# The down projection of a gated feed-forward block by Strassen's algorithm, with its operand sums made ahead in the gate and up passes

## The chip, the core and the metric

The kernel runs on one core of one Trainium2 chip. The time is device microseconds of one execution: 2796.57 us, the median of 3 runs (2796.07 to 2796.67). A separate execution was profiled; it took 2792.36 us.

## The reference

One layer of a hybrid trunk over 16 meta tokens and 2048 tokens of width 1024, all in 32-bit floating point: a token mixer (a state-space branch and an mLSTM branch, merged and projected), and then a channel mixer. Only the channel mixer, and in it the last product, matters here:

```python
def channel_mixer(x, g_pre, g_post, w_gate, w_up, w_conv, b_conv, w_down):
    h = rmsnorm(x, g_pre)
    a = causal_dwconv(h @ w_gate, w_conv, b_conv)
    y = (jax.nn.gelu(a, approximate=True) * (h @ w_up)) @ w_down
    return x + rmsnorm(y, g_post)
```

The inner width is 2816, 22 blocks of 128 features. Shapes of the down projection: y is 2048 x 2816, w_down 2816 x 1024. The result is normalized over all 1024 features of a token, multiplied with g_post and added to x.

## The kernel before

TensorE multiplies 32-bit numbers in a rounded form (fp32r). To keep the precision, every operand is split into a high part, which ACT rounds (an activation Copy into an fp32r tile), and a low part, the rest, which DVE subtracts. Each product is then three matmuls: high x high, high x low, low x high (`mm3`, lines 172 to 174; `mm3x`, lines 177 to 179, is the same without a check on groups). So each operand tile costs a load, an ACT and a DVE instruction before TensorE can use it.

All DMAs of the kernel are issued by SP, one after the other, in SP's own order. Each waits there until its buffer is free or its data is written, and what stands behind it waits as well. The program text gives the dependencies and the buffers (a pool's tile with `bufs=2` has two buffers that take turns); a scheduler sets the order of each engine's instructions.

The channel mixer has two parts.

**Gate and up passes** (`ffn_unit`, called in two loops over the 22 feature blocks m; first for the token half p=0, then for p=1). Gate and up are computed together by Strassen's algorithm in Winograd's form: seven products in the order 1, 6, 2, 7, 5, 4, 3 in place of eight, each of 4 depth blocks. Their seven operand tiles of h lie in SBUF throughout a pass (t0 to t11, q0, q1, from `t4(i)` and `q4(i)`). The weights of a unit are loaded (wg at line 1131, wu at 1133, buffer `ws` of pool dw), summed on DVE (s1 to s4) and split (lines 1124, 1125). In pass p=0 the moving operand has 258 or 256 columns (two pieces whose products alternate), in pass p=1 512. Behind the products come sums in u1 to u3 and gp (DVE), a causal convolution along tokens (ACT line 1254, DVE line 1256 twice), gelu (ACT line 1257), the product with the up half (DVE line 1261), and a store into `y_d` (line 1262) in DRAM, twice a unit.

**Down projection** (after `phX.close()`). For each half nh of the output features (512 columns) the weights w_down of all 22 depth blocks lie in SBUF, split (loaded into tiles `mk`, split at lines 1328 and 1329 into the t tiles). Then over 16 token tiles i: three loads `ys` from y_d of 8, 8 and 6 depth blocks (line 1335), each split into `yhl` (lines 1338 and 1339), and 22 x 3 matmuls into one PSUM bank with y as the stationary operand and 512 columns of weights moving. ys and each part of yhl have two buffers. A square sum (ACT line 1345) and a product with g_post (DVE, 1347 or 1350) follow. The results of nh=0 stay in SBUF; with nh=1 the token is normalized, h1 is loaded and added, and the output stored (1355 to 1359).

## Time and profile before

| | |
|---|---|
| median of 3 runs | 2796.57 us |
| profiled execution, its time / its span | 2792.36 us / 2790.6 us |
| TensorE busy (PE) | 2759.1 us, 99% |
| DVE / ACT busy | 1761.1 us, 63% / 1054.7 us, 38% |
| gate and up, pass p=0 | from 1403.8 us to about 1850 us |
| gate and up, pass p=1 | from there to about 2290 us |
| down projection, first and last matmul | 2287.3 us, 2783.3 us |
| DMA traffic | 395.47 MB, mean 142 GB/s |

PE are TensorE's matmuls and PEld its weight loads, which overlap them. The duration of a single matmul is longer than the distance of two, since they are pipelined; the pace is read from counts over a stretch of time. DVE is VectorE, ACT ScalarE, POOL GpSimd, SP SyncE, whose queue issues the DMAs. In a row of a group there stand line, engine, operation, output and inputs by their names in the program, shapes and count, then busy time in us and mean ns of one, then idle time before it and what ended most of it.

### The profile page before, as it was taken

To read this page: it belongs to the slowest core of one execution; us is meant where nothing else is said; L and a number is where in the kernel's file an instruction comes from. 1 tells how busy PE (TensorE), PEld (TensorE's weight loads), DVE (VectorE), ACT (ScalarE), POOL (GpSimd) and SP (SyncE) were. 2 spreads that over 40 slices of the span, in tenths; PEclk is the share of its full clock that TensorE was granted. 3 is DMA by queue.
4 is the path that set the end of the run, shared out by engine and by line. 5 is a ranking of instruction groups with operands and counts; after the bars stand their busy time and mean duration, and the time that the engine had idled before them with its cause. 6 is when DMAs were issued, how large, how long until landed. Compare 5 with 4: busy or idle time off the path is not lost.

```text
span 2790.6 us, 40815 instructions
## 1 busy us (share of the span) xinstructions
PE 2759.1 (99%) x15590; PEld 2484.9 (89%) x15590; DVE 1761.1 (63%) x3429; ACT 1054.7 (38%) x1979; POOL 136.8 (5%) x225
## 2 busy tenths in 40 slices
PE   8999999999999999999999999999999999999999
PEld 8999999999999987777799999998788788888887
DVE  4637799377555464676798887786776683224333
ACT  6102344233444444344354434453443352224221
POOL 1000000000000000000100000000000000000000
PEclk9999999999999999999999999999999999999999
DMA  9333443212454574667744462252222244335453
GB/s 309 106 79 131 158 147 121 71 69 72 145 159 144 167 212 121 223 196 250 265 157 138 159 234 87 73 176 85 80 80 81 79 145 149 99 90 165 157 166 128
DMA packets 323478, 395.47 MB, mean 142 GB/s; under 512 B 40321, under 2 KB 229142, under 8 KB 322642
## 3 DMA queue, kind: packets, MB, share of 16 engines
q1 hardware_dynamic: 323282, 392.86, 43.9%
q8 instruction: 122, 2.00, 0.3%
q14 instruction: 74, 0.61, 0.1%
HBM read 284.47 MB, written 108.31 MB: 141 GB/s over the span
## 4 chain that ended last, share of the span: by engine, by line
PE 82%; DMA 7%; DVE 6%; ACT 1%; issue 1%; POOL 1%; SPq 0%; DVEq 0%; POOLq 0%; ACTq 0%
PE mm L172 10%; PE mm L174 10%; PE mm L173 10%; PE ac L173 9%; PE ac L174 9%; PE ac L172 8%; PE ac L179 4%; PE ac L178 4%; PE ac L177 4%; PE mm L177 3%; PE mm L179 3%; PE mm L178 3%; DMA wu<-in_w_up_dram 2%; DMA gat<-gab_d 1%; DVE w L1125 1%
## 5 line engine op out<-in xcount | busy, mean ns | idle before, releaser
L174 PE MATMUL mm<-hTh,wl 128*128 128x410 f32 (+3 forms) x1216 | 428.0, 352 | 0.0
L172 PE MATMUL mm<-hTh,wh 128*128 128x410 f32 (+3 forms) x1216 | 427.6, 352 | 0.0
L173 PE MATMUL mm<-hTl,wh 128*128 128x410 f32 (+3 forms) x1216 | 427.4, 352 | 0.0
L1339 DVE TENSOR_TENSOR yhl<-ys,yhl 128x1024 fp32r<-128x1024 f32 (+1 forms) x96 | 109.1, 1137 | 291.9 <-ACT yhl L1338 291.9
L173 PE MATMUL ac<-t,yhl 128*128 128x512 f32 x704 | 278.5, 396 | 0.0
L174 PE MATMUL ac<-t,yhl 128*128 128x512 f32 x704 | 277.3, 394 | 0.0
L172 PE MATMUL ac<-t,yhl 128*128 128x512 f32 x704 | 276.6, 393 | 0.0
L177 PE MATMUL mm<-t,w 128*128 128x258 f32 (+2 forms) x792 | 253.7, 321 | 3.5 <-DVE u L1226 2.6
L178 PE MATMUL mm<-t,w 128*128 128x258 f32 (+2 forms) x792 | 253.5, 320 | 0.4 <-DVE t L1069 0.4
L177 PE MATMUL ac<-t,w 128*128 128x258 f32 (+2 forms) x792 | 253.2, 320 | 0.6 <-ACT u L1217 0.6
L179 PE MATMUL ac<-t,w 128*128 128x258 f32 (+2 forms) x792 | 253.1, 320 | 0.1
L179 PE MATMUL mm<-t,w 128*128 128x258 f32 (+2 forms) x792 | 252.5, 320 | 0.7 <-DVE w L1125 0.7
L178 PE MATMUL ac<-t,w 128*128 128x258 f32 (+2 forms) x792 | 253.1, 320 | 0.0
L173 PEld LDWEIGHTS mm<-hTl,wh 128*128 128x128 f32 x1216 | 228.7, 188 | 2.6
L174 PEld LDWEIGHTS mm<-hTh,wl 128*128 128x128 f32 x1216 | 228.8, 188 | 2.3
L172 PEld LDWEIGHTS mm<-hTh,wh 128*128 128x128 f32 x1216 | 228.7, 188 | 2.0
L1338 ACT ACTIVATE yhl<-ys 128x1024 fp32r<-128x1024 f32 (+1 forms) x96 | 95.0, 990 | 348.4 <-PE ac L173 345.9
L156 ACT ACTIVATE wh<-ws 128x1024 fp32r<-128x1024 f32 x104 | 109.9, 1059 | 237.8 <-PE mm L173 137.5
L1124 ACT ACTIVATE w<-s 128x512 fp32r<-128x512 f32 x176 | 109.3, 628 | 164.7 <-DVE s L1139 70.3
L177 PEld LDWEIGHTS mm<-t,w 128*128 128x128 f32 x792 | 149.7, 189 | 18.0 <-DVE u L1226 4.4
L172 PEld LDWEIGHTS ac<-t,yhl 128*128 128x128 f32 x704 | 132.4, 188 | 32.3
L177 PEld LDWEIGHTS ac<-t,w 128*128 128x128 f32 x792 | 149.2, 189 | 13.0 <-ACT u L1217 1.1
(453 smaller groups left out, 6074.1 us busy)
## 6 DMA issues: line engine op xcount, KB each, us to landing
ys<-y_d SPq DMA_DIRECT2D x64, 512.0 KB, 3.7
wg<-in_w_gate_dram SPq DMA_DIRECT2D x44, 512.0 KB, 3.6
wu<-in_w_up_dram SPq DMA_DIRECT2D x44, 512.0 KB, 4.3
gab_d<-ev SPq DMA_DIRECT2D x80, 205.0 KB, 2.4
ws<-in_w_m_dram SPq DMA_DIRECT2D x32, 512.0 KB, 3.8
ws<-in_w_ba_dram SPq DMA_DIRECT2D x32, 512.0 KB, 4.0
ws<-in_w_out_dram SPq DMA_DIRECT2D x32, 512.0 KB, 5.3
gat<-gab_d SPq DMA_DIRECT2D x48, 256.0 KB, 4.8
```

Of the source, the lines that this page charges most:

```text
L156: S.activation(wh, ws, AF.Copy, scale=scale)
L172: T.matmul(out=ps, lhsT=lh, rhs=rh, start=first, stop=False)
L173: T.matmul(out=ps, lhsT=lh, rhs=rl, start=False, stop=False)
L174: T.matmul(out=ps, lhsT=ll, rhs=rh, start=False, stop=last)
L177: T.matmul(out=ps, lhsT=lh, rhs=rh, start=first, stop=False, skip_group_check=True)
L178: T.matmul(out=ps, lhsT=lh, rhs=rl, start=False, stop=False, skip_group_check=True)
L179: T.matmul(out=ps, lhsT=ll, rhs=rh, start=False, stop=last, skip_group_check=True)
L1124: S.activation(t[:, 0], src, AF.Copy)
L1125: V.tensor_tensor(t[:, 1], src, t[:, 0].bitcast(F32), ALU.subtract)
L1338: S.activation(yh, ys, AF.Copy)
L1339: V.tensor_tensor(yl, ys, yh.bitcast(F32), ALU.subtract)
```

## The change

The down projection becomes one Strassen step (Winograd's form, as in gate and up), over y in quarters: two token groups of 128 (j and j+4 of a pass), and the depth in two halves of 11 blocks. A `down_unit` computes two token tiles by 512 features with seven products, each of 11 depth blocks x 3 matmuls with 256 moving columns. There are 8 units for each feature half nh, so 2 x 8 x 7 products.

Three of the seven operands of y are parts of y itself, four are sums, and so it is for the weights. The sums are made earlier and put in DRAM: those of the weights (`down_weight_sums`, into `wt_d`) in the first gate and up pass, one call in each of the units m = 9 to 20, two loads, four DVE sums and four stores; those of y (`down_input_sums`, into `s_d`) in the second pass, one call in each of the units m = 1 to 11 and 13 to 21, again two loads of 512 KB from y_d, four DVE sums of 128x512 and four stores of 256 KB. For two of the depth blocks the sums of the second token half are made within the down projection, after its second and third unit (j = 1 and 2; `late_sums`).

For every feature half the seven weight operands lie in SBUF, 8 of their 11 depth blocks in the t and q tiles (`main`), 3 in tiles x1 to x7 (`rest`). For nh=0 the mains of five products are loaded and split within the last gate and up unit (`turn_down`), the other two and all rests in the first down unit; those of nh=1 in the last unit of nh=0 and the first of nh=1 (the table `cut`). Each stationary operand (704 KB), each main piece, each rest piece and the late sums use one tag `raw` with two buffers in the new pool dn, which takes over the space of dw, mk, du and dx. The results of nh=0 go to DRAM (`yo_d`) and are loaded again by `finish`.

```diff
+    def down_weight_sums(nh, k):
+        kn = min(2, 11 - k)
+        t = mk_tile()[:, 0:kn * 1024].rearrange("p (k b n) -> p k b n", k=kn, b=4)
...
+        V.tensor_tensor(b11, b12, b11, ALU.subtract)
...
+    def down_input_sums(p, m, t1, t2):
+
+        for h, t in ((0, t1), (1, t2)):
+            P.dma_start(out=t, in_=y_d[m + 11 * h, :, p * 1024:(p + 1) * 1024])
+        a11, a21, a12, a22 = t1[:, 0:512], t1[:, 512:1024], t2[:, 0:512], t2[:, 512:1024]
+        V.tensor_tensor(a22, a21, a22, ALU.add)
+        V.tensor_tensor(a21, a11, a21, ALU.subtract)
+        V.tensor_tensor(a11, a22, a11, ALU.subtract)
+        V.tensor_tensor(a12, a12, a11, ALU.subtract)
+        for i, a in enumerate((a11, a21, a12, a22)):
+            P.dma_start(out=s_d[p * 4:p * 4 + 4, i, :, m, :].rearrange("j p t -> p j t"),
+                        in_=a.rearrange("p (j t) -> p j t", j=4))
...
+        if 9 <= m < 21:
+            down_weight_sums((m - 9) // 6, (m - 9) % 6 * 2)
...
     for m in range(NF):
         if m:
             wt = weights_second(*weights(m))
-        ffn_unit(1, m, op1, wt)
+        i = m - 1 if m < 12 else m - 13
+        if i >= 0 and i < (11 if m < 12 else 9):
+            t = mk_tile()
+            down_input_sums(int(m > 12), i, t[:, 0:1024], t[:, 1024:2048])
+        ffn_unit(1, m, op1, wt, turn_down if m == NF - 1 else None)
     phX.close()
+    phM.close()
+    phW.close()
...
+    dn = pool(ctx, "dn")
+
+    def raw_tile():
+        return dn.tile([128, 1408], F32, tag="raw", name="raw", bufs=2)
...
+    def stationary(j, n):
+        raw = raw_tile()
+        src3 = raw.rearrange("p (m t) -> p m t", m=11)
+        if n in (1, 2, 4):
+            c0 = j // 4 * 1024 + j % 4 * 128 + 512 * (n == 4)
+            m0 = 11 * (n != 1)
+            P.dma_start(out=src3, in_=y_d[m0:m0 + 11, :, c0:c0 + 128].rearrange("m p t -> p m t"))
+        else:
+            P.dma_start(out=src3, in_=s_d[j, {6: 0, 7: 1, 3: 2, 5: 3}[n]])
+        turn_[0] += 1
+        st = dn.tile([128, 2, 1408], F32R, tag=f"st{turn_[0] % 2}", name="st")
+        S.activation(st[:, 0], raw, AF.Copy)
+        V.tensor_tensor(st[:, 1], raw, st[:, 0].bitcast(F32), ALU.subtract)
+        return st.rearrange("p a (m t) -> p a m t", m=11)
...
+        def prod(ps, n, first):
+            for f in before.get(n, ()):
+                f()
+            st = ahead.pop(n, None) or stationary(j, n)
+            for k in range(11):
+                mm3x(ps, st[:, 0, k], st[:, 1, k], moving(n, 0, k), moving(n, 1, k), first and k == 0, k == 10)
...
+    def second(n):
+        return [lambda: main_piece(1, n, 0), lambda: main_piece(1, n, 4), lambda: rest_split(1, n)]
+
+    todo = [f for n in ORDER for f in second(n)]
+
+    cut = [0, 0, 1, 3, 5, 6, 8, 9, 12, 14, 16, 18, 20, 21]
+    for j in range(8):
+        if j == 0:
+            before = first
+        elif j == 7:
+            before = {n: todo[cut[i - 1] if i else 0:cut[i]] for i, n in enumerate(ORDER)}
+        else:
+            before = {}
+        down_unit(0, j, g4, before)
+        if j in (1, 2):
+            late_sums(8 + j)
```

How the order of SP's queue changes, at two places. Rows show line, the tile written and the one read; waits are named by the engine that gives the semaphore (DVE, Activation, PE) or by the DMA queue's (DMAHW). Line numbers of the changed program differ: y_d<-cc is line 1262 before and 1297 after, wg 1131 and 1166, wu 1133 and 1168.

The first place is the second gate and up pass. Before, a unit's rows on SP are these four:

```order
L1262 DMA y_d<-cc 128x512 [waits DMAHW2_49,DVE_49]
L1262 DMA y_d<-cc 128x512 [waits DMAHW3_49,DVE_49]
L1131 DMA wg<-in_w_gate_dram 128x1024 [waits DMAHW0_49,DVE_49,Activation_49]
L1133 DMA wu<-in_w_up_dram 128x1024 [waits DMAHW1_49,DVE_49]
L1262 DMA y_d<-cc 128x512 [waits DMAHW6_49,DVE_49]
```

After, in a unit past the twelfth (mk<-y_d are the loads of y for the sums, s_d<-mk the stores of the sums):

```order
L1297 DMA y_d<-cc 128x512 [waits DMAHW5_49,DVE_49]
L1147 DMA mk<-y_d 128x1024 [waits DMAHW5_49,DMAHW3_49]
L1154 DMA s_d<-mk 128x4x128 [waits DMAHW6_49,DVE_49]
L1166 DMA wg<-in_w_gate_dram 128x1024 [waits DVE_49,Activation_49]
L1154 DMA s_d<-mk 128x4x128 [waits DVE_49]
L1154 DMA s_d<-mk 128x4x128 [waits DMAHW2_49,DVE_49]
L1154 DMA s_d<-mk 128x4x128 [waits DVE_49]
```

A load that waits for DMA queues only (its own y block must have been stored) and a store of a sum now stand between the store of y and the load of the next unit's wg.

The second place is the beginning of the down projection. Before, the loads of y (ys) stand among the last stores of the gate and up units:

```order
L1335 DMA ys<-y_d 128x8x128 [waits DMAHW4_49,DVE_49,Activation_49]
L1322 DMA mk<-in_w_down_dram 128x4x512 [waits DVE_49]
L1335 DMA ys<-y_d 128x8x128 [waits DMAHW5_49,DMAHW2_49,DVE_49]
L1262 DMA y_d<-cc 128x512 [waits DMAHW3_49,DVE_49]
L1322 DMA mk<-in_w_down_dram 128x4x512 [waits DVE_49]
L1335 DMA ys<-y_d 128x6x128 [waits DMAHW0_49,DVE_49]
L1322 DMA mk<-in_w_down_dram 128x2x512 [waits DMAHW6_49,DVE_49]
L1262 DMA y_d<-cc 128x512 [waits DMAHW7_49,DVE_49]
```

After, the first load of a stationary operand (raw<-y_d) stands behind the last three stores, and the loads that follow go to the two raw buffers in turn:

```order
L1297 DMA y_d<-cc 128x512 [waits DVE_49] x3
L1397 DMA raw<-y_d 128x11x128 [waits DMAHW6_49,PE_49]
L104 DMA g_23166<-in_g_ffn_post_dram 128x512
L1399 DMA raw<-s_d 128x1408 [waits DMAHW0_49,PE_49]
L1495 DMA ht<-h_d 128x512 [waits DMAHW3_49,DMAHW1_49,Pool_49]
L1495 DMA ht<-h_d 128x512 [waits DMAHW2_49]
L1411 DMA raw<-in_w_down_dram 128x3x256 [waits DMAHW6_49,DVE_49]
L1411 DMA raw<-wt_d 128x768 [waits DMAHW4_49,DMAHW0_49,DVE_49]
L1411 DMA raw<-in_w_down_dram 128x3x256 [waits DMAHW5_49,DMAHW3_49,DVE_49]
L1397 DMA raw<-y_d 128x11x128 [waits DMAHW4_49,DVE_49]
L1411 DMA raw<-wt_d 128x768 [waits DMAHW7_49,DMAHW5_49,DVE_49]
L1399 DMA raw<-s_d 128x1408 [waits DMAHW6_49,DVE_49]
```

Rests (line 1411) and stationaries (1397, 1399) alternate; every raw load from the third on waits for DVE, which reads the buffer last.

More of the change, by code (lines that the diff above doesn't have):

```diff
@@ L86, in mixer_ffn_kernel @@
     y_d = dp.tile([NF, 128, 2048], F32, name="y_d")
+    s_d = dp.tile([8, 4, 128, 11, 128], F32, name="s_d")
+    wt_d = dp.tile([2, 4, 128, 11, 256], F32, name="wt_d")
+    yo_d = dp.tile([16, 128, 512], F32, name="yo_d")
     win_d = dp.tile([8, 128, 512], F32, name="win_d")
@@ L858, in mixer_ffn_kernel @@
         mlstm(pool(ph, "ml", bufs=2))
-    mk = pool(ctx, "mk")
+    phM = ExitStack()
+    mk = pool(phM, "mk")
     def mk_tile(dt=F32):
@@ new lines, in rest_tile, with rest_split, main_piece @@
+    def rest_tile(n):
+        wrest[n] = dn.tile([128, 2, 768], F32R, tag=f"x{n}", name=f"x{n}")
+    def rest_split(nh, n):
+        raw = raw_tile()[:, 0:768]
+        P.dma_start(out=raw.rearrange("p (k n) -> p k n", k=3), in_=down_src(nh, n, 8, 11))
+        rest_tile(n)
+        S.activation(wrest[n][:, 0], raw, AF.Copy)
+        V.tensor_tensor(wrest[n][:, 1], raw, wrest[n][:, 0].bitcast(F32), ALU.subtract)
+    def main_piece(nh, n, k0):
+        raw = raw_tile()[:, 0:1024]
+        P.dma_start(out=raw.rearrange("p (k n) -> p k n", k=4), in_=down_src(nh, n, k0, k0 + 4))
+        if k0 == 0:
+            places(n)
+        main_split(n, k0, raw.rearrange("p (a n) -> p a n", a=2))
@@ new lines, in finish @@
+    def finish(t, o1):
+        sm = dn.tile([128, 1], F32, tag="sm", name="sm", bufs=2)
+        V.tensor_reduce(out=sm, in_=sq4[t], op=ALU.add, axis=mybir.AxisListType.X)
+        rs = rstd_of(Small(dn, "r", 2), sm, 128, 1, 1.0 / D)
+        o0 = dn.tile([128, 512], F32, tag="o", name="o0", bufs=3)
+        P.dma_start(out=o0, in_=yo_d[t])
+        for hh, src in ((0, o0), (1, o1)):
+            cs_ = slice(hh * 512, hh * 512 + 512)
+            ht = dn.tile([128, 512], F32, tag="ht", name="ht", bufs=2)
+            P.dma_start(out=ht, in_=h1_d[NM + t * 128:NM + (t + 1) * 128, cs_])
+            V.scalar_tensor_tensor(ht, src, rs, ht, ALU.mult, ALU.add)
+            P.dma_start(out=out[t * 128:(t + 1) * 128, cs_], in_=ht)
@@ new lines, in late_main, with late_sums @@
+    def late_main(n):
+        for k0 in (0, 4):
+            main_piece(0, n, k0)
+    ahead = {1: stationary(0, 1)}
+    g4 = half_gains(0)
+    ahead[6] = stationary(0, 6)
+    rest_split(0, 1)
+    rest_split(0, 6)
+    first = {n: [lambda n=n: rest_split(0, n)] for n in ORDER[2:]}
+    for n in ORDER[5:]:
+        first[n].insert(0, lambda n=n: late_main(n))
+    def late_sums(m):
+        down_input_sums(1, m, raw_tile()[:, 0:1024], raw_tile()[:, 0:1024])
+    def second(n):
+        return [lambda: main_piece(1, n, 0), lambda: main_piece(1, n, 4), lambda: rest_split(1, n)]
@@ new lines, in mixer_ffn_kernel @@
+    todo = [f for n in ORDER for f in second(n)]
[5 more added lines that the diff above has]
+            before = {n: todo[cut[i - 1] if i else 0:cut[i]] for i, n in enumerate(ORDER)}
+        else:
+            before = {}
+        down_unit(0, j, g4, before)
+        if j in (1, 2):
+            late_sums(8 + j)
+    g4 = half_gains(1)
+    for j in range(8):
+        before = {n: todo[cut[6 + i]:cut[7 + i]] for i, n in enumerate(ORDER)} if j == 0 else {}
+        down_unit(1, j, g4, before)
```

133 lines of the change are left out of this document (82 added, 51 removed).

## The prediction

> **What bounds the kernel now.** I read the page first: its engine table and its stretch table say who is busy.
>
> ```profile
> span 2790.6 us, 40815 instructions
> PE 2759.1 (99%) x15590; PEld 2484.9 (89%) x15590; DVE 1761.1 (63%) x3429; ACT 1054.7 (38%) x1979; POOL 136.8 (5%) x225
> ```
>
> TensorE is busy throughout, so less TensorE work pays only as long as everything that feeds it keeps its place. Next the busy times by stretch (length; PE, PEld, DVE, ACT, POOL busy with instructions in brackets; granted clock; DMA share; GB/s): 40 and 160 us of the gate and up pass over the first token half (moving operands of 256 to 258 columns), 100 us of the pass over the second half (512 columns), and two stretches of the down projection (512).
>
> ```profile
> 1723.00:1763.00 40.00, 40.00 (x337) 40.00 (x336) 30.12 (x58) 16.92 (x30) 0.37 (x2) 1.00 0.25 80
> 1643.00:1803.00 160.00, 160.00 (x1339) 160.00 (x1339) 122.74 (x236) 67.70 (x121) 2.02 (x9) 1.00 0.28 92
> 1943.00:2043.00 100.00, 99.10 (x425) 79.70 (x424) 70.33 (x113) 41.47 (x68) 4.56 (x5) 1.00 0.27 85
> 2310.00:2500.00 190.00, 190.00 (x820) 153.64 (x819) 50.29 (x51) 43.42 (x61) 0.00 (x0) 1.00 0.35 105
> 2500.00:2780.00 280.00, 280.00 (x1207) 226.43 (x1206) 110.13 (x154) 75.77 (x112) 8.28 (x15) 1.00 0.48 155
> ```
>
> Counts give the pace: 40/337 = 0.1187 us for a narrow matmul (the longer stretch has gaps in its records) and 470/2027 = 0.2319 us for a wide one. Half the columns cost 51% of the time. Then the feed of the down projection: who waits for whom around its input tiles, and their costs.
>
> ```profile
> L1339 DVE TENSOR_TENSOR yhl<-ys,yhl 128x1024 fp32r<-128x1024 f32 x63 | 77.2, 1226 | 227.7 <-ACT yhl L1338 227.7
> L1338 ACT ACTIVATE yhl<-ys 128x1024 fp32r<-128x1024 f32 x62 | 65.8, 1061 | 230.1 <-PE ac L173 230.1
> L1339 DVE TENSOR_TENSOR yhl<-ys,yhl 128x768 fp32r<-128x768 f32 x32 | 30.7, 959 | 64.2 <-ACT yhl L1338 64.2
> L1338 ACT ACTIVATE yhl<-ys 128x768 fp32r<-128x768 f32 x32 | 27.1, 848 | 115.8 <-PE ac L173 115.8
> ```
>
> ACT waits for PE before nearly every split (346 us in all): the feed is early, TensorE is last. One input tile is loaded, split high, split low: 3.7 + 1.06 + 1.23 = 6.0 us, two tiles in flight, so one per 3.0 us, while TensorE takes 24 x 0.2319 = 5.6 us over it. That factor of nearly two is what the change spends.
>
> ```profile
> ys<-y_d SPq DMA_DIRECT2D x64, 512.0 KB, 3.7
> ys<-y_d SPq DMA_DIRECT2D x32, 384.0 KB, 3.2
> mk<-h_d SPq DMA_DIRECT2D x8, 1026.0 KB, 4.9
> mk<-h_d SPq DMA_DIRECT2D x12, 512.0 KB, 3.1
> y_d<-cc SPq DMA_DIRECT2D x44, 256.0 KB, 4.0
> out_dram<-ht SPq DMA_DIRECT2D x32, 256.0 KB, 2.2
> ```
>
> **The change part by part.** The sum is made against the profiled execution, 2792.4 us (span 2790.6); the median shown is 2796.6, 0.15% above it, and I carry the difference over.
>
> *TensorE: -51 us.* Out go 16 x 2 x 22 x 3 = 2112 wide matmuls, 2112 x 0.2319 = 489.8. In come 2 x 8 x 7 x 11 x 3 = 3696 narrow ones, as many as the first gate and up pass has; at 0.1187 that is 438.7, or 27.4 us for a unit of seven products and 3.92 for a product.
>
> *What one use of the load buffer costs.* Everything the down projection reads now passes through two raw buffers: 112 stationaries (704 KB) and, of weights, 18 main pieces (512 KB) and 14 rest pieces (384 KB). SP issues a load when DVE has finished with the buffer two uses before (the last fence of the part on the change). So a use holds its buffer for load + high split + low split. Splits of 1408 columns, along the two widths above: ACT 1.06 + 384 x 0.21/256 = 1.40 (0.848 to 1.061 is 0.21, and the shortest row of 768 would give 0.04 less), DVE 1.23 + 384 x 0.267/256 = 1.63. Loads: an input of 704 KB in 512-byte runs like ys: 3.7 + 192 x 0.5/128 = 4.45; from the sums, in long runs like mk from h_d: 3.1 + 192 x 1.8/514 = 3.8; main piece between 3.1 and 3.7, so 3.4; rest piece between 2.7 and 3.2, so 3.0. A use is then 7.5 (input), 6.8 (sum), 5.7 (main), 4.8 (rest). In an ordinary unit the three inputs and four sums cost (3 x 7.5 + 4 x 6.8)/2 = 24.9 of TensorE's 27.4: hidden, with 10% to spare. In three units it isn't.
>
> *First unit: +41 us.* Before, the first ys was loaded while the last gate and up unit ran, and TensorE went through without a gap. Now (same fence) the first raw load is behind the last three y_d stores, and these behind the end of the last unit's chain, with the last product just done:
>
> ```profile
> L1236 DVE TENSOR_TENSOR gp<-ac,u 128x512 f32<-128x512 f32 x1 | 0.7, 691 | 0.0
> L1254 ACT ACTIVATE cc<-gp,cbf,cwf 128x512 f32<-128x512 f32 x2 | 1.6, 820 | 5.6 <-DVE gp L1236 5.5
> L1256 DVE SCALAR_TENSOR_TENSOR cc<-gp,cwf,cc 128x512 f32<-128x512 f32 x4 | 3.0, 750 | 1.3 <-ACT cc L1254 1.3
> L1257 ACT ACTIVATE cc<-cc 128x512 f32<-128x512 f32 x2 | 1.3, 635 | 0.5 <-DVE cc L1256 0.4
> L1261 DVE TENSOR_TENSOR cc<-cc,u 128x512 f32<-128x512 f32 x3 | 2.1, 687 | 0.0
> L1335 SPq DMA_DIRECT2D ys<-y_d x96: 359/366/378, 2274.0 to 2766.4; - x96
> ```
>
> 0.69 + 0.82 + 2 x 0.75 + 0.64 + 0.69 + 0.37 for SP's own issue = 4.7 us, then load and high split, 4.45 + 1.40: TensorE stands still for 10.6 us. The unit has 18 uses (7 stationaries, 7 rests, 4 mains), 106 us of buffer time, 53 in two buffers. Followed one by one in SP's order, each low split behind the one before it and each stationary behind the product two before it, the last product ends 68 us after the last one of the gate and up pass; 68 - 27.4 = 41. Without the queueing it would be 4.7 + 53 + 3.9 = 62 (+34).
>
> *Turn of the halves: +54 us.* In the last unit of the first half and the first of the second all 14 mains and 7 rests of the second half's weights are loaded beside 14 stationaries: 14 x 7.1 + 14 x 5.7 + 7 x 4.8 = 213, halved 106.5; I take 109 for the strict alternation, against 54.8 of TensorE.
>
> *Late sums: +26 us.* After units 1 and 2 a pair of y rows takes both raw buffers: load (3.4), four DVE sums (4 x 0.69 = 2.8), stores (4 issues and a landing, 3.5), and only then the next stationary: load and split 5.9. 15.6 us, of which TensorE has 4.6 in hand, and 1.6 more for its third matmul, which needs the low split: 13 each, twice.
>
> *Second half: +10 us.* A unit moves 7 x 704 KB and ten transfers of 256 KB, 7.7 MB in 27.4 us, 280 GB/s. The trace has 342 GB/s with the DMA full (row below), so the queues are some 80% busy and a stationary is at times behind a store or two of 0.75 us; 0.3 of slack at an input's use: I take 1.5 us a unit for seven units.
>
> *Gate and up passes: +12 us.* DVE gets 12 x 4 sums in the first pass and 20 x 4 in the second, 2.8 us a unit. In the first pass it is 77% busy (row above) and TensorE bounds. In the second the four sums stand where DVE waits for wg:
>
> ```profile
> L1125 DVE TENSOR_TENSOR w<-wg,w 128x512 fp32r<-128x512 f32 x39 | 26.8, 691 | 62.8 <-ACT w L1124 59.1 <-PE ac L179 3.7
> SPq L1131 <- DVE s L1192: 60.8, 19, 5.7
> ```
>
> 62.8 us of idle time in 19 units covers 2.8 each. But SP has two loads and four stores more to issue, and wg is now behind a store of sums (the second fence there). From the thirteenth unit on, the second load reads what the unit two before stored, so SP may stand until that store has landed (4.0), and DVE's first sum until the load has (3.4). Ends: nothing, and 7.4 x 9 = 67 us; I take 0.6 us a unit, near the lower end, since in the old order wg had 3.2 us of waiting on SP per unit.
>
> Sum: -51 + 41 + 54 + 26 + 10 + 12 = +92. 2792.4 + 92 = 2884; on the scale of the median 2889.
>
> The rows of 512 KB land in 3.1 and 3.7 us. [...]
>
> **The rivals.**
>
> *Loads land later everywhere.* Where other transfers were in flight, at the start of the old down projection, ys landed at:
>
> ```profile
> DMA to landing us min/median/max: 3.8/5.2/6.6
> ```
>
> With 5.2 for all stationaries a use is 8.2 and a product 4.1, 0.2 above TensorE's 3.92: 77 ordinary products lose 15, and 53 uses in the three crowded units some 1.3 us each in one of two buffers, 34: 2938. For it: two raw loads are always in flight. Against: the median over the whole stage is 3.7.
>
> *The sums disturb the second pass* by the whole SP wait in its last nine units (7.4 less the 3.2 of slack, 38) and the 0.6 in the eleven before: 44 in place of 12, 2921. The weights of a unit are loaded only once the unit before has released them, so there is no reserve.
>
> *TensorE falls to half clock in the gaps.* This trace shows that once before the passes:
>
> ```profile
> 1271.57 0.50 PE L172 MATMUL ac<-wh,t 128*128 128x512 f32 x1 [2.03 <-ACT o L1016]
> 1272.00:1277.00 5.00, 5.00 (x17) 3.87 (x16) 2.80 (x4) 3.17 (x5) 1.07 (x2) 0.66 1.03 342
> ```
>
> After 2.0 us of idling the clock was halved for some 3.4 us. 21 products in the crowded units with such a gap would lose 1.7 us each, 36; half of it under the loads that bound there: 2907. The Trainium skill ("TensorE: Matmul & The Clock Gate", Part 1) has the rule, half clock after an idle window of about 3.4 us; by that length fewer gaps would count.
>
> *It ends faster: the loads are hidden after all.* The place is the first unit and the turn, the price 41 + 54 + 26. If they cost nothing, 2796.6 - 51 + 22 = 2768; the kernel breaks even when those three cost 29 together. For it: DMA shares of 0.28 to 0.48 leave room. Against: the two splits alone hold the buffers (7 x 3.03 + 7 x 1.81 + 4 x 2.29)/2 = 21.5 of the first unit's 27.4 us, so loads would have to land in 0.65 us; the shortest landing quoted is 2.2.
>
> **How the numbers follow.** The forecast (2889, its own range 2865 to 2915) 57%; late loads 16%; disturbed second pass 12%; half clock 9%; hidden loads 4%; the losses there about half as large, 2835, 2%. The range leaves out the hidden loads and the far ends: 2848 to 2945. Slower by over 0.2% (about what this kernel's timing can tell from no change) 95%, within it 1%, faster 4%.
>
> **What would show it.** TensorE's matmul count in the last stage 3696, its busy share there clearly under 1 in three places: the first 70 us, 42 us for each of the units with late sums, some 110 us around the turn; in between 27 to 29 us a unit. SP's longest waits should be for DVE's low split, ACT's for DMA landings in place of PE. The second pass should keep 19.5 to 20.5 us a unit. A stage without those holes would make the forecast wrong; so would a unit that takes over 30 us without extra loads.

## The result and the profile after

The changed kernel takes 2941.3 us (median of 4 runs, 2940.4 to 2947.1) against 2796.6 us before: a ratio of 1.052, with a 95% interval of 1.0502 to 1.0538. The forecast was 2889, its own range 2865 to 2915, and the range over the rivals 2848 to 2945. So the direction and three holes in the last stage came as described, but the loss is 145 us and not 92, above the forecast's own range. The profiled execution of the change took 2941.0 us, with a span of 2939.0; the sums below compare it with the span of 2790.6 before.

The first lines of the page after. TensorE's busy share falls from 99% to 94%, although TensorE has less to do:

```profile
span 2939.0 us, 45045 instructions
...
PE 2770.7 (94%) x17174; PEld 2569.1 (87%) x17174; DVE 1966.5 (67%) x3691; ACT 1142.5 (39%) x2073; POOL 132.2 (4%) x225
```

Next the same table by stretch that the prediction began with: length; PE, PEld, DVE, ACT, POOL busy, with instructions in brackets; granted TensorE clock; DMA share; GB/s. First the kernel before: the two gate and up passes, and the down projection from the last product of the passes on.

```profile
1403.80:1862.30 458.50, 455.29 (x3775) 452.61 (x3774) 378.71 (x707) 209.72 (x372) 19.89 (x34) 1.00 0.43 141
1862.30:2302.10 439.80, 437.39 (x1876) 352.18 (x1875) 320.34 (x511) 186.94 (x309) 30.77 (x23) 1.00 0.31 99
2302.10:2783.70 481.60, 481.60 (x2074) 389.13 (x2072) 165.20 (x211) 123.34 (x179) 8.28 (x15) 1.00 0.43 137
```

Then the change: the two passes; the first unit of the down projection; the second; the third and the fourth, each behind a late pair of sums; three ordinary units; the two units of the turn; the seven units of the second half. The last addition of a unit (line 1478, 16 times, from 2406.8 to 2928.7 us) marks its end.

```profile
1405.70:1872.70 467.00, 458.99 (x3775) 454.66 (x3774) 401.40 (x756) 209.11 (x373) 23.56 (x34) 1.00 0.56 189
1872.70:2329.00 456.30, 437.35 (x1835) 346.63 (x1833) 363.45 (x573) 180.18 (x292) 23.02 (x23) 0.99 0.56 179
2329.00:2406.80 77.80, 41.64 (x234) 39.00 (x234) 31.63 (x34) 24.61 (x29) 0.00 (x0) 0.71 0.53 168
2406.80:2434.30 27.50, 27.49 (x231) 27.28 (x230) 14.78 (x17) 10.24 (x15) 0.00 (x0) 1.00 0.56 185
2434.30:2474.70 40.40, 29.86 (x231) 29.36 (x231) 17.65 (x21) 11.72 (x16) 0.00 (x0) 0.87 0.58 190
2474.70:2515.30 40.60, 30.02 (x233) 29.73 (x234) 17.75 (x21) 13.02 (x18) 0.00 (x0) 0.87 0.61 193
2515.30:2598.30 83.00, 82.89 (x695) 82.60 (x694) 44.68 (x50) 34.72 (x49) 0.00 (x0) 1.00 0.64 203
2598.30:2720.20 121.90, 78.95 (x465) 73.69 (x463) 54.29 (x58) 44.33 (x54) 0.55 (x1) 0.79 0.59 183
2720.20:2928.70 208.50, 197.77 (x1617) 193.47 (x1615) 123.70 (x167) 80.14 (x111) 7.71 (x14) 1.00 0.74 249
```

An undisturbed unit takes 27.5 us, as forecast (27.4); the units behind late sums 40.4 and 40.6 (forecast 40.4). The first unit takes 77.8 (68), the turn 121.9 (109), the second half 29.8 a unit (28.9). In none of these stretches is the DMA full, and TensorE's clock is down in the crowded ones: 0.71 over 77.8 us means 45 us at half clock, and 117 us in the whole stage. The two passes, which were to lose 12, are 25 us longer, and that although 40 matmuls of the down projection (9.3 us) ran in the second of them before and do not any more.

The splits of the load buffer cost what the prediction took for them, and the landings, read from the DMA issues (KB each, median us from issue to landing), are longer for the sums: 4.4 us in place of 3.8.

```profile
L1403 DVE TENSOR_TENSOR st<-raw,st 128x1408 fp32r<-128x1408 f32 x112 | 182.0, 1625 | 175.4 <-ACT st L1402 175.2
...
L1402 ACT ACTIVATE st<-raw 128x1408 fp32r<-128x1408 f32 x112 | 154.5, 1380 | 249.0 <-DMA raw<-s_d 88.0
...
raw<-s_d SPq DMA_DIRECT2D x64, 704.0 KB, 4.4
raw<-y_d SPq DMA_DIRECT2D x48, 704.0 KB, 4.5
```

ACT waited for PE before the change; now its largest waits in the stage are for landings, and SP's are for DVE's low split, which frees the buffer (engine and line, what it waited for: us in all, times, longest):

```profile
ACT st L1402 <- DMA raw<-s_d: 88.0, 34, 5.8
ACT st L1402 <- DMA raw<-y_d: 85.3, 26, 7.3
```
```profile
SPq L1399 <- DVE st L1403: 62.4, 27, 4.7
SPq L1397 <- DVE st L1403: 56.3, 19, 3.3
```

One use of a buffer in the turn, from the timeline (start, us, engine and line): the load is issued at 2659.96, the high split starts at 2664.14, the low split at 2665.55; it ends at 2667.17, and 0.03 us later SP issues the next load into this buffer.

```profile
2659.96 0.32 SPq L1399 DMA_DIRECT2D raw<-s_d  x1
...
2664.14 1.38 ACT L1402 ACTIVATE st<-raw 128x1408 fp32r<-128x1408 f32 x1 [2.99 <-DMA raw<-s_d]
...
2665.55 1.62 DVE L1403 TENSOR_TENSOR st<-raw,st 128x1408 fp32r<-128x1408 f32 x1 [3.41 <-ACT st L1402]
...
2667.20 0.32 SPq L1418 DMA_DIRECT2D raw<-wt_d  x1
```

That is the two-buffer chain of the prediction, link by link. The same chain can be followed through the turn: by share of its 121.9 us, what the work that ended last went through there (landings, splits, TensorE; the row is cut at its end by the view).

```profile
by line: DMA raw<-s_d 16.2%; DMA raw<-y_d 16.0%; DMA raw<-wt_d 14.7%; ACT st L1402 10.2%; DVE st L1403 10.2%; issue 5.6%; DMA raw<-in_w_down_dram 5.1%; DMA out_dram<-ht 4.5%; DVE t L1359 4.0%; ACT t L1358 2.6%; DVE x L1414 2.4%; ACT x L1413
```

TensorE is on it for one product alone, 6.3 us near the end. The experiments ask whether the two buffers, the halved clock or the transfers set the time, and what happened in the passes. All ratios below are against the kernel before, run beside the experiment on the same chip; its medians there were 2796.9 to 2800.6 us.

### The profile page after: what moved, and what is told of

The parts are those of the page before. It is cut to its first block, busy times and chain, and to the rows that moved or that the text cites. A ratio compares the mean times of both kernels' runs of the same rounds, so it can differ in the third digit from the quotient of the medians.

```text
span 2939.0 us, 45045 instructions
## 1 busy us (share of the span) xinstructions
PE 2770.7 (94%) x17174; PEld 2569.1 (87%) x17174; DVE 1966.5 (67%) x3691; ACT 1142.5 (39%) x2073; POOL 132.2 (4%) x225
## 4 chain that ended last, share of the span: by engine, by line
PE 55%; DMA 23%; DVE 15%; ACT 3%; issue 2%; POOL 1%; SPq 1%; ACTq 0%; DVEq 0%; POOLq 0%
PE mm L175 9%; PE mm L176 9%; PE mm L177 9%; DMA raw<-s_d 3%; DMA raw<-y_d 3%; DMA wu<-in_w_up_dram 3%; PE ac L176 3%; PE ac L177 3%; PE ac L175 3%; PE ac L182 3%; PE ac L180 2%; PE ac L181 2%; DVE w L1160 2%; DVE st L1403 2%; PE mm L182 2%
## 5 line engine op out<-in xcount | busy, mean ns | idle before, releaser
L1403 DVE TENSOR_TENSOR st<-raw,st 128x1408 fp32r<-128x1408 f32 x112 | 182.0, 1625 | 175.4 <-ACT st L1402 175.2
L180 PE MATMUL mm<-t,w 128*128 128x258 f32 (+2 forms) x792 | 257.7, 326 | 14.4 <-DVE u L1261 6.3
L181 PE MATMUL mm<-t,w 128*128 128x258 f32 (+2 forms) x792 | 256.1, 324 | 0.7 <-DVE t L1074 0.7
L182 PE MATMUL mm<-t,w 128*128 128x258 f32 (+2 forms) x792 | 254.7, 323 | 1.0 <-DVE w L1160 1.0
L1402 ACT ACTIVATE st<-raw 128x1408 fp32r<-128x1408 f32 x112 | 154.5, 1380 | 249.0 <-DMA raw<-s_d 88.0
L180 PEld LDWEIGHTS mm<-t,w 128*128 128x128 f32 x792 | 151.4, 191 | 33.5 <-DVE u L1261 6.4
L180 PEld LDWEIGHTS ac<-t,w 128*128 128x128 f32 x792 | 149.4, 189 | 23.6 <-ACT w L1159 9.8
L180 PE MATMUL ac<-t,st 128*128 128x256 f32 x384 | 116.9, 304 | 49.2 <-ACT st L1402 49.2
L182 PEld LDWEIGHTS mm<-t,w 128*128 128x128 f32 x792 | 151.1, 191 | 13.7 <-DVE w L1160 1.7
L181 PEld LDWEIGHTS mm<-t,w 128*128 128x128 f32 x792 | 151.5, 191 | 12.3 <-DVE t L1074 0.9
L182 PEld LDWEIGHTS ac<-t,w 128*128 128x128 f32 x792 | 149.4, 189 | 13.9 <-DVE w L1160 2.6
L181 PEld LDWEIGHTS ac<-t,w 128*128 128x128 f32 x792 | 149.7, 189 | 11.4
```

Of the source, the lines that this page charges most:

```text
L180: T.matmul(out=ps, lhsT=lh, rhs=rh, start=first, stop=False, skip_group_check=True)
L181: T.matmul(out=ps, lhsT=lh, rhs=rl, start=False, stop=False, skip_group_check=True)
L182: T.matmul(out=ps, lhsT=ll, rhs=rh, start=False, stop=last, skip_group_check=True)
L1402: S.activation(st[:, 0], raw, AF.Copy)
L1403: V.tensor_tensor(st[:, 1], raw, st[:, 0].bitcast(F32), ALU.subtract)
```

## Experiments on the down projection

**More loads in flight.** Three kernels share one edit in three sizes. In place of a third buffer of 1408 columns the pieces were made smaller: `raw4` has four buffers of 768 columns, `raw3h` three, `raw6` six of 512.

```
-        return dn.tile([128, 1408], F32, tag="raw", name="raw", bufs=2)
+        return dn.tile([128, 768], F32, tag="raw", name="raw", bufs=4)
...
+        for m1, mn in ((0, 6), (6, 5)):
+            raw = raw_tile()[:, 0:mn * 128]
...
```

> The two load buffers of 1408 columns become four of 768: a stationary is loaded and split in two pieces (6 and 5 depth tiles), a main weight piece in two of 512 columns, a late pair of rows in four. Nearly the same space, the same work, twice the loads in flight. Theory 'buffers' (the length of the crowded units is load plus two splits, shared by the buffers): a half use holds a buffer for about 3.2 + 0.75 + 0.9 = 4.9 us, so a stationary costs 2.45 us of buffer time in place of 3.9; first unit 78 to about 58 us after the last gate and up product, the two units of the turn 122 to about 82, second half 29.8 to 27.5 us a unit: about 2870. Rival 'transfers' (the loads are slow because the DMA queues are shared, so that more of them in flight only land later): the landings of the half loads rise to 4.5 us or more, and the time falls by under 25: 2916 or more. Rival 'clock' (the halved TensorE clock sets the length of those units): the gaps shrink but stay over 2 us, so that no more than 20 are won: 2920.

> Three load buffers of 768 columns (2304 columns in all, less than the change's two of 1408) with the half pieces; all else as with four of 768. It tells the number of loads in flight from the bytes in flight. Theory 'buffers': a piece holds its buffer 5.0 to 5.2 us (768 or 704 columns) or 4.3 (512), and three share it; first unit 140/3 + 18 = 65 us (four: 52.9), turn 296/3 + 12 = 110 (four: 86.6), ordinary units 27.5 to 28.5: 2887 on a scale where four give 2850. Rival 'bytes in flight': with 18% fewer bytes in flight than the change it is as slow as the change or slower, 2941 or more.

> Six load buffers of 512 columns, the same bytes as four of 768; a stationary comes in three pieces, a rest piece in two. Theory 'buffers': a piece holds its buffer 3.1 + 0.55 + 0.65 = 4.3 us, shared by six: 0.72 us for 512 columns in place of 0.86; first unit 48 us, turn 76: 2835 on a scale where four give 2850. Rival 'transfers': the turn moves 20.2 MB, which takes 59 us at the 342 GB/s that the trace of the kernel before shows with the DMA full, and the DMA share was 0.8 with four buffers; then the pieces land later in place of sooner (256 KB in 3.8 us or more) and the time stays at 2847 or more.

Measured: three of 768 columns 1.0402 (1.0387 to 1.0418), four 1.0192 (1.0174 to 1.0209), six of 512 1.013 (1.0107 to 1.0154), against 1.052 of the change. Here are the first unit and the turn of three, of four and of six buffers, in this order:

```profile
2321.40:2386.90 65.50, 40.53 (x238) 37.45 (x238) 33.03 (x46) 27.64 (x42) 0.00 (x0) 0.79 0.65 196
2569.90:2679.00 109.10, 74.29 (x473) 69.33 (x473) 57.90 (x85) 49.46 (x82) 1.34 (x1) 0.83 0.66 201
```
```profile
2319.80:2372.70 52.90, 34.50 (x234) 32.88 (x234) 32.32 (x45) 26.68 (x41) 0.00 (x0) 0.81 0.76 237
2554.60:2641.20 86.60, 69.00 (x465) 65.56 (x464) 55.37 (x83) 48.01 (x81) 0.00 (x0) 0.86 0.80 250
```
```profile
2325.20:2378.40 53.20, 36.57 (x234) 34.23 (x234) 33.70 (x60) 28.51 (x56) 0.00 (x0) 0.81 0.79 247
2554.60:2635.00 80.40, 66.25 (x475) 62.29 (x474) 57.80 (x106) 51.98 (x104) 0.79 (x1) 0.92 0.87 272
```

The turn goes from 121.9 to 109.1, 86.6 and 80.4 us with two, three, four and six loads in flight, the first unit from 77.8 to 65.5, 52.9 and 53.2. Three buffers were expected to give 65 and 110. This kernel has fewer bytes in its buffers than the change and does the same work, so it is not the bytes in flight that bound, and more loads in flight help. "Transfers" falls for the change: the DMA was 0.59 busy in its turn, against 0.87 with six. "Clock" falls as the main cause: with six buffers the turn is 41 us shorter, while its time at half clock fell from 51 to 13 us, which is worth 19 us at most. What the sum missed: the three-buffer kernel's second half stayed slow (216.7 us for seven units; four buffers 195.3, six 192.3), so that it came out 21 us above its expectation. And with six buffers the second rival is half right: the DMA is 0.87 busy in the turn at 272 GB/s, the landings did not shorten further (medians of 3.4 to 4.3 us for 256 KB, against 3.1 expected), the first unit won nothing, and the turn 6 us of the 11 expected; the total is the expected one only because the late sums and the second half won 9 us more. From there on the transfers themselves seem to bound; no run tests it.

**The halved clock.** Matmuls that compute nothing were put into TensorE's gaps; in the second version each group is tied to its place.

```
+            count = 0
+            if (nh, j) in ((0, 0), (0, 7), (1, 0)):
+                count = 92 if nh == 0 and j == 0 and n == 1 else 25
+            elif nh == 0 and j in (2, 3) and n == 1:
+                count = 70
+            queue = tc.issue_after(keep_busy(count).ins) if count else nullcontext()
...
+        with tc.issue_after(newest[0].ins):
+            for q in range(count):
+                added = T.matmul(out=ps, lhsT=warm[:, 0:128], rhs=warm, start=True, stop=True, skip_group_check=True)
```

> Matmuls that compute nothing are put into TensorE's gaps, into a spare PSUM tile: 92 before the first product of the down projection, 25 (3 us) before each product of the first unit and of the two units of the turn, 70 before the first product of the two units that follow late sums. Nothing else changes. In the changed kernel 327 of the down projection's matmuls start at half clock, 0.213 us apart in place of 0.119, which is 31 us of TensorE time. Theory 'buffers': in the crowded units the next load is issued by the low split, not by TensorE, so a faster product only waits longer; what is won is the restart after the long gaps, 2 to 3 us in each of the two late-sum units: 2933 to 2937. Rival 'clock': those 31 us are on the path, and the time falls to about 2910. If the added matmuls themselves delay products, it is 2941 or more, with the gaps filled and the clock at full.

> The added matmuls once more, now each group tied to its place: issued behind the last matmul of the product before and ahead of the first of its own product (the products of the down projection are thereby strictly one behind the other). Same groups: 92 ahead of the first product, 25 ahead of each further product of the first unit and of the two units of the turn, 70 ahead of the first product of the units behind late sums. Theory 'buffers': clock at full in those units, and yet they take 77.8 and 121.9 less at most 3 us each, since loads set them; the two late-sum units lose 2 to 3 us each: about 2932 to 2938. Rival 'clock': first unit 10, turn 17, late-sum units 3.5 us shorter: 2910.

The first version took 1.0577 (1.056 to 1.0594), since the planner (the scheduler of the program text), free to move matmuls that wait for nothing, drew the groups of the turn into the units 1 to 6: an ordinary unit there has 280 matmuls and takes 33 us. So it says nothing of the turn. The tied version took 1.0539 (1.0515 to 1.0562), the time of the change. Its first unit and its turn:

```profile
2320.80:2397.50 76.70, 63.79 (x475) 62.89 (x476) 31.00 (x33) 25.01 (x31) 0.00 (x0) 0.89 0.54 173
2592.00:2715.10 123.10, 108.20 (x814) 105.66 (x813) 54.20 (x58) 43.98 (x53) 0.55 (x1) 0.92 0.57 179
```

The time at half clock falls from 45 to 17 us in the first unit and from 51 to 20 in the turn (one less the granted clock, times two, times the length), and the two take 76.7 and 123.1 us, as without the added matmuls (77.8 and 121.9). This alone does not show that the halved clock costs nothing: TensorE waited for the high split of a stationary before 7 of these 21 products only (14.7 us in all), and the other 14 began straight behind the added matmuls, which may have taken what the faster clock gave. The trace of the change bounds the price. On the chain that ended last, TensorE stands for 11.2 us of the first unit (two products) and 6.3 us of the turn (one), of these 7.4 and 5.3 us at half clock; everything else is landings, splits and issues. So the half clock costs some 6 us at most in the two (an estimate, half of 12.7), of the 50 and 67 us that they lose: as a rule a product that is done sooner waits longer for its next stationary. The two late-sum units did not get the 2 to 3 us shorter that "buffers" expected (42.5 and 40.7 us).

**The turn and the late sums by themselves.**

```
-            before = {n: todo[cut[i - 1] if i else 0:cut[i]] for i, n in enumerate(ORDER)}
+            before = {}
...
-        before = {n: todo[cut[6 + i]:cut[7 + i]] for i, n in enumerate(ORDER)} if j == 0 else {}
+        before = {}
```

> The second half of the features uses the weights of the first, which are not loaded or split again (left out: the second half's weights). The turn then holds two ordinary units. Theory 'buffers': 121.9 us become 27.5 + 28 to 30, so 63 to 66 us are won: 2877. The units of the second half keep their 29 to 30.5 us, since their transfers of rows, not the turn, slow them. Rival: that the second half is slow because it starts late behind the turn: its units go to 27.5 as well, 2862. Half clock should be gone from the turn in both.

```
-            P.dma_start(out=src3, in_=s_d[j, {6: 0, 7: 1, 3: 2, 5: 3}[n]])
+            P.dma_start(out=src3, in_=s_d[j % 4, {6: 0, 7: 1, 3: 2, 5: 3}[n]])
...
-        if j in (1, 2):
-            late_sums(8 + j)
```

> The sums of the last two pairs of rows are not made after units 1 and 2 of the down projection; the units of the second token half read the sums of the first half at the same addresses less the token half (left out: the second token half's sums in the down projection). Theory 'buffers': units 2 and 3 go from 40.3 and 40.6 us to 27.5, which wins 26: 2915. Within these 26, 20 are standstill of TensorE and the rest the restart at half clock, so a rival by which the standstill alone counts and the next units have spare time for the rest gives 2921.

Measured 1.0299 (1.0275 to 1.0323) and 1.0433 (1.0412 to 1.0454): 62 and 24 us less than the change on the scale of 2796.6. The two units of the turn without new weights, and the third and fourth unit without late sums, one row of each kernel:

```profile
2591.80:2647.90 56.10, 55.76 (x466) 55.29 (x465) 29.78 (x35) 23.34 (x33) 0.00 (x0) 1.00 0.68 209
```
```profile
2425.00:2480.20 55.20, 55.20 (x466) 55.20 (x466) 29.82 (x33) 23.17 (x33) 0.00 (x0) 1.00 0.66 203
```

Both holes close to ordinary units at full clock, so the 67 us of the turn and the 26 us of the late sums are the weights and the sums, but for about 1 us of the turn. The time alone can't separate the 26 us from the rival's 20; the trace does. The second half kept its 30 us a unit without the turn (212.5 us for seven), so the turn does not cause that.

**The second half.** A third buffer for the rows of the output stage:

```
-            ht = dn.tile([128, 512], F32, tag="ht", name="ht", bufs=2)
+            ht = dn.tile([128, 512], F32, tag="ht", name="ht", bufs=3)
```

> A third buffer for the rows of the output stage in the second half (2 KB a partition that were free). Theory: a unit of the second half takes 29.8 us in place of 27.5 because SP, which issues all transfers in order, stands at the load of such a row until the store two before it has landed (29.7 us in 23 waits there), and the next stationary's load is queued behind it: with three that wait goes, and the second half wins 5 to 12 us: 2929 to 2936. Rival 'traffic' (the transfers of rows themselves, or SP's waits for DVE ahead of the out stores, 38.2 us in 15 waits, which stay): 2939 to 2941, units unchanged at 29 to 30.5.

Measured 1.0511 (1.0492 to 1.053), no different from the change; the seven units took 212.9 us. SP's waits in the second half, first the change, then this kernel:

```profile
SPq L1497 <- DVE ht L1496: 38.2, 15, 11.3
SPq L1495 <- DMA out_dram<-ht: 29.7, 23, 4.2
```
```profile
SPq L1495 <- DMA out_dram<-ht: 44.5, 28, 4.5
SPq L1497 <- DVE ht L1496: 22.5, 9, 11.4
```

The theory fell: SP stands for the landing of the output rows as before, even longer, and the waits for DVE ahead of the out stores fell, but not to nothing. What is shown is that the second half loses 2.3 us a unit with two load buffers, 3.5 with three, 0.4 with four and nothing with six. The chain that ended last there, by share of the 208.5 us, is again that of the two buffers, and SP's stand for the landing of output rows (`out_dram<-ht`) is a part of it:

```profile
by line: DMA raw<-s_d 24.5%; DMA raw<-y_d 18.1%; DVE st L1403 14.5%; ACT st L1402 12.6%; DMA out_dram<-ht 11.4%; issue 3.4%; DVE ht L1496 2.2%; POOL rs L110 1.6%; PE ac L182 1.4%; PE mm L182 1.4%; DVE o L1455 1.3%; DMA ht<-h_d 1.2%; PE ac L
```

And the sums landed later there than in the three ordinary units of the first half (the trace ties six landings to their loads there, three here; the second half stands first):

```profile
DMA to landing us min/median/max: 4.1/5.2/6.1
```
```profile
DMA to landing us min/median/max: 3.9/3.9/4.5
```

From the issue of the load to the end of the low split, sums held their buffer for 8.5 us in the second half and inputs for 7.9, against 7.8 and 7.9: (4 x 8.5 + 3 x 7.9)/2 = 29 us a unit, near the 29.8 measured. How the loss divides between these landings and SP's stand for the stores stays open.

## Experiments on the passes

**The sums alone**, on the kernel before:

```
+        if 9 <= m < 21:
+            down_weight_sums((m - 9) // 6, (m - 9) % 6 * 2)
...
     for m in range(NF):
...
+        i = m - 1 if m < 12 else m - 13
+        if i >= 0 and i < (11 if m < 12 else 9):
+            t = mk_tile()
+            down_input_sums(int(m > 12), i, t[:, 0:1024], t[:, 1024:2048])
         ffn_unit(1, m, op1, wt)
```

> The kernel before with the sums of the weights and of the rows added to its gate and up passes as in the change; its down projection is the old one and does not read them, and the down projection's weights are not loaded within the last unit. Theory 'the sums disturb both passes': pass one 8 to 9 us longer than before (458.5 to 467), pass two 14 to 17 us (439.8 to 456), so 1.8 to 2.5% of a pass and 22 to 27 us in all: 0.8 to 0.95% slower than before. Rival: that a good part of the change's 25 us in the passes came from what else stands there (the weights loaded within the last unit, the code placed elsewhere): under 12 us here, under 0.45% slower.

Measured 1.0113 (1.0094 to 1.0132), 32 us, 5 more than the upper end of what was expected; so nothing but the sums is needed for what the passes lose. Its two passes:

```profile
1404.20:1866.90 462.70, 456.24 (x3775) 452.89 (x3774) 401.26 (x755) 208.63 (x373) 22.56 (x34) 1.00 0.57 190
1866.90:2333.30 466.40, 447.47 (x1884) 355.50 (x1883) 370.41 (x591) 186.08 (x309) 24.69 (x23) 0.99 0.59 185
```

The first pass loses 4 us (8.5 in the profiled execution of the change, 3.5 to 6.5 in those of the eight experiments whose passes are the change's), the second 27. In the change the second is only 16.5 us longer than before, since the down projection's matmuls no longer run in it: here 48 of them still do, 11.1 us. The expectation was made from the passes of the change and did not have them. Why the second loses so much is in the trace of the change: the first row counts the first additions of the eleven groups of the first token half, the others are SP's waits between 1872.7 and 1980 us, and TensorE's largest gap in a pass.

```profile
L1149 DVE TENSOR_TENSOR mk<-mk x11: 684/693/696, 1882.5 to 1964.3; 128x512 f32<-128x512 f32 x11
```
```profile
SPq L1147 <- DMA s_d<-mk: 24.4, 11, 4.8
```
```profile
1949.76 0.80 PE L180 MATMUL ac<-t,w 128*128 128x512 f32 x1 [6.39 <-ACT w L1159]
```

All eleven groups run within the first 100 us of the pass. The planner drew them ahead, since nothing held them, and not one to a unit as the loop is written. Their loads (line 1147) share three buffers with the stores of the groups before (line 1154), and SP, which issues in order, stood for these landings with the next unit's weights queued behind.

**The sums tied to their units:**

```
-        P.dma_start(out=wu, in_=w_up[m])
+        newest[0] = P.dma_start(out=wu, in_=w_up[m])
...
-            down_weight_sums((m - 9) // 6, (m - 9) % 6 * 2)
+            with tc.issue_after(newest[0].ins):
+                down_weight_sums((m - 9) // 6, (m - 9) % 6 * 2)
...
-            down_input_sums(int(m > 12), i, t[:, 0:1024], t[:, 1024:2048])
+            with tc.issue_after(newest[0].ins):
+                down_input_sums(int(m > 12), i, t[:, 0:1024], t[:, 1024:2048])
```

> The sums in the passes are tied to their units: each unit's loads for sums are queued on SP behind that unit's load of wu, so that one pair of rows (or one weight group) belongs to each unit, as the code is written. In the changed kernel the planner had drawn the eleven groups of the first token half ahead: all of them ran within the first 100 us, five units of the second pass, and TensorE lost 6.4 us at one place there and 6.8 us at half clock. Nothing else changes. Theory 'bunching': a good part of the second pass's 25 us of TensorE time comes from those five units (15.6 us longer than before) and goes: second pass 8 to 14 us shorter, 2927 to 2933, ratio to the kernel before 1.047 to 1.049. Rival 'each group costs the same wherever it stands' (SP's four stores and two loads, 25/20 = 1.25 us a unit): the pass keeps its length, 2941, 1.052.

Measured 1.0464 (1.0448 to 1.048). The third addition of a group (line 1151 there) now runs five times in the first 100 us, and the second pass takes 444.7 us in place of 456.3:

```profile
L1151 DVE TENSOR_TENSOR mk<-mk x5: 674/682/687, 1882.5 to 1963.7; 128x512 f32<-128x512 f32 x5
```
```profile
1866.00:2310.70 444.70, 432.70 (x1836) 345.93 (x1834) 362.34 (x574) 179.19 (x294) 29.00 (x23) 0.99 0.57 183
```

So 12 us of the second pass were the bunching. What is left is the sums at one group to a unit: before, the pass took 439.8 us with 9.3 us of the down projection's matmuls in it (below), so 430.5 without them, and 14 us more now. That is 0.7 us for each of the 20 groups, where the prediction had taken 0.6. The first pass took 462.2 us with its weight sums tied as well, as it did untied in the other experiments (462.0 to 465.0), so bunching is not what it loses by.

**Both together, and the late sums in small pieces.** The first kernel has the edits of `raw6` and of the tied sums; the second has these and

```
...
-        if j in (1, 2):
-            late_sums(8 + j)
...
+        elif j in (1, 2):
+            before = {n: [lambda n=n: late_sums(8 + j, ORDER[::2].index(n))] for n in ORDER[::2]}
```

> Six load buffers of 512 columns together with the tied sums. The two act in different stages, so the gains should add: 1.013 less 0.3 to 0.5% is 1.008 to 1.010 of the kernel before under 'bunching', 1.013 under the rival. It is not expected to be faster than the kernel before: with ordinary units everywhere (16 x 27.5 = 440 us against 490 before) 50 us would be won, and what is left of the first unit (25 over an ordinary one), the turn (25), the late sums (10) and the passes (15 to 28) is more.

> Six buffers, the tied sums, and now the late sums in eight small pieces: each takes one load buffer (the four blocks of 128 columns of a pair of rows), two loads, four sums of 128 columns and one store, and stands ahead of every other product of the units 1 and 2, in place of two sets that take four buffers at once between units. Theory: units 2 and 3 go from 32.8 us to 28 to 29, the units 1 and 2 lose at most one: 6 to 10 us won, 1.0045 to 1.006 of the kernel before. Rival (each small piece holds its buffer as long as a large one, and the pieces' store lands late): the units 1 and 2 grow by what units 2 and 3 win, 1.008. Not faster than the kernel before in either: the first unit and the turn alone keep 50 us more than ordinary units, which is all that the narrower work wins.

Together they took 1.0079 (1.0059 to 1.0099): the gains add as expected. The small late sums, eight sets of 128 columns ahead of the products of the units 1 and 2, took 1.0094 (1.0077 to 1.0111), the same. The three units from the second on, first without and then with them:

```profile
2360.00:2454.40 94.40, 88.02 (x695) 86.99 (x694) 52.55 (x98) 39.43 (x90) 0.00 (x0) 0.95 0.74 227
```
```profile
2362.40:2455.70 93.30, 84.80 (x689) 83.56 (x688) 53.12 (x119) 40.68 (x90) 0.00 (x0) 0.98 0.75 225
```

Unit 1 grew from 28.7 to 34.1 us and unit 3 fell from 32.8 to 27.5: the rival was right, since a small piece takes a buffer out of the same row of uses. No kernel here beats the one before. The best has 25 us too many in the first unit, 25 in the turn, 12 around the late sums and 15 in the passes, against the 51 that the narrower matmuls bring (for these two see the next section).

## Why the prediction was right, and where its sum was off

The mechanism in the down projection was right, and "hidden loads" (2768) was wrong by the step it named: the loads can't land fast enough for two buffers. The sum of 92 was short by 56 in the profiled execution, so the measured time lies above the forecast's own range; that it lies within the wide one (2848 to 2945) is in part luck, since that range was drawn for the rivals and not for terms that are all too small. Measured by the tables above, term by term, in one execution each (in other executions of the same stages the first pass was up to 5 us shorter and the second half up to 5 us longer):

| term | forecast | measured | from |
|---|---|---|---|
| TensorE's work | -51 | -51 | 481.6 + 9.3 to 16 x 27.5 = 440.0 |
| first unit | +41 | +50 | 77.8 - 27.5 |
| turn of the halves | +54 | +67 | 121.9 - 55.0 |
| late sums | +26 | +26 | 81.0 - 55.0 |
| second half | +10 | +16 | 208.5 - 192.5 |
| gate and up passes | +12 | +34 | 8.5 and 16.5 + 9.3 |
| start, three ordinary units, tail | 0 | +6 | 1.9, 0.5, 3.4 |
| sum | +92 | +148 | 2939.0 - 2790.6 |

*TensorE.* The term was right. Of the 2112 wide matmuls 40 had run before the last product of the gate and up passes; at 0.2319 us they are 9.3 us, and the table counts them with the down projection. They did not run in gaps. Before, TensorE was busy without a break around them, from the first of the 40 (2287.3 us) to behind the last product of the pass (2302.1):

```profile
2287.00:2310.00 23.00, 23.00 (x101) 18.63 (x100) 19.51 (x30) 14.30 (x25) 0.13 (x1) 1.00 0.91 299
```

And the kernel with the sums alone, in which 48 of them (11.1 us) still run in the second pass, has a pass of 466.4 us, 10 us longer than the change with the same sums (456.3, and 453.7 to 458.2 in the eight experiments with the same passes). So taking them out won nearly their full time, and the second pass lost 25.8 us to the sums where the ends of the passes show 16.5.

*First unit and turn.* The step that failed is the cost of a use: 6.8 us for a stationary of sums, 7.5 for one of inputs, 5.7 for a main piece. From the issue of the load to the end of the low split, the 34 uses of the turn took 8.0, 8.3 and 6.4 us on average (the one shown above 7.2). The splits were right to 0.02 us. What was off is the landing. That of the sums was taken from a load of h_d in long runs that had landed in 3.1 us for 512 KB; long runs brought nothing here (4.4 against 4.5 us in runs of 512 bytes). In the turn the inputs came late too: the two landings that the trace ties to their loads there took 5.1 and 5.2 us, in place of 4.45. The rest are low splits and splits that stood behind other work on DVE and ACT. With 14 stationaries at 1.0 us more each, 14 mains at 0.7 and 7 rests at 0.4, over two buffers, that is 13 us, the whole miss of the turn. In the first unit the same, and 2 us more standstill: 12.5 us in place of 10.6, since SP issued the first load 6.3 us after the last product and not 4.7:

```profile
2335.31 0.38 SPq L1397 DMA_DIRECT2D raw<-y_d  x1
...
2341.48 0.58 PE L180 MATMUL ac<-t,st 128*128 128x256 f32 x1 [12.46 <-ACT st L1402]
```

*Passes.* The step that failed is "the four sums stand where DVE waits for wg", one group to a unit. For the first token half the planner's order had eleven groups in five units; "2.8 us a unit" was then 6 us a unit, and SP's waits for the landing of stores, priced for the last nine units only, came in the first five too. That cost 12 of the 26 us of the second pass; the other 14, one group to a unit, are about what the prediction took. The first pass, costed at nothing because TensorE bounds it, lost 3.5 to 8.5 us to the weight sums; by which wait stays open.

*The rivals.* "Late loads everywhere" gave 2938, the nearest number, but that is luck: it took 15 us from ordinary products, while ordinary units of the first half stayed at 27.5 us, and it left the passes at 12. It was right in part: landings of 5.2 us came in the turn and in the second half. "The sums disturb the second pass" was right in kind, and for this pass its 44 us were too much by 18. "Half clock" was wrong in its price: it was on for 117 us of the stage, where the rival had counted 21 gaps of 3.4, 71 us, but in the first unit and the turn the path went through TensorE at half clock for 13 us only. The Trainium skill ("TensorE: Matmul & The Clock Gate", Part 1) has the half clock behind an idle window of about 3.4 us; the trace agrees on the step, since the stretches at half clock in its record of the clock come in multiples of 3.41 us, and the rule says nothing on whether TensorE is what the path waits for. On the idle time it does not agree: the standstill of 2.03 us in the prediction's own row was enough, so gaps shorter than 3.4 us count. (The trace before shows that twice before the passes and not once: the granted clock is 0.66 from 1375 to 1380 us as well, behind a standstill of 2.95 us.)

*What would have shown it wrong* came in part. The signs for the down projection held: 3696 matmuls, busy shares under 1 in the three places named, SP waiting for DVE's low split and ACT for landings, no slow unit without extra loads in the first half. But four of the seven units of the second half took over 30 us without loads of weights or late sums (28.9 was forecast), and the second pass did not keep 19.5 to 20.5 us a unit: it took 20.7 on average, and more in its first five units.

## What to carry to other kernels

A staging buffer is held from the issue of its load to the end of its last reader, so price a stage as (uses x hold) / buffers, with the hold from a trace in which as many loads are in flight, and compare that with the compute it must hide under, in the crowded units and not on average. Where it is short, try smaller pieces in more buffers of about the same total size: here that won until the DMA was 0.87 busy. Before a halved clock is given a price, look whether the chain that ends last goes through TensorE at all. Work that "fits in the gaps" of another stage has to be looked up in the planner's order. And where the planner moves work across the border of two stages, count it with the same stage before and after.

## What was not expected of the hardware

Within one kernel a smaller load landed hardly sooner: with four buffers 256 KB of weights took 3.0 to 3.3 us, 320 KB 3.5 to 3.9 and 384 KB 3.4 to 3.5, with six 192 KB took 3.5 to 4.2 and 256 KB 3.4 to 4.3 (medians by source). With two buffers 704 KB took 4.4 to 4.5; from kernel to kernel size and number in flight changed together. The DMA share of the turn rose from 0.59 to 0.87 and its rate from 183 to 272 GB/s with 3072 columns of buffers in place of 2816. And TensorE at half clock for 45 of the 78 us of the first unit cost some 4 us at most, an estimate from its share of the chain that ended last.
